# Attention scores of a hybrid encoder block: q_hi times k_lo of two heads on the two halves of TensorE's rows

## The chip, the cores and the metric

The kernel runs on one NeuronCore of a Trainium2 chip. The metric is the device time of one launch in microseconds (us), taken as the median of three runs. TensorE is called PE below, its weight loads PEld, VectorE is DVE, ScalarE is ACT, GpSimd is POOL and SyncE is SP.

## What is computed

One encoder layer on x of 1 x 1024 x 1024 in float32, with 8 query heads, 2 key/value heads and a head width of 64:

```
h = rmsnorm(x);  q | k | v | u = h @ w_in
q = axial_rope(rmsnorm(q));  k = axial_rope(rmsnorm(k))
s = q . k * 64**-0.5;  a = softmax(s) . v          # per 128-query block and head
p = pool_mixer(u)
x = x + concat([a, p]) @ w_out
x = x + (silu(h2 @ w_gate) * (h2 @ w_up)) @ w_down # h2 = rmsnorm(x)
```

The softmax runs over all 1024 keys; four query heads share one key/value head. D_FF is 2816.

## The kernel before

All matmuls take operands in a rounded 32-bit form (fp32r). To keep float32 accuracy each operand is split in a high part (the rounded value) and a low part (what is left), and a product is made of hi.hi, hi.lo and lo.hi. A matmul streams 512 columns through 128 rows.

For the scores, the split is stacked in the 128 rows instead: a head is 64 wide, so a query tile holds q_hi in rows 0 to 63 and q_lo in rows 64 to 127 (`prep_q` splits, `turn_q` transposes on PE and ACT copies the result out of PSUM, L804). The key side, `kT[:, kv, b, :]`, holds k_hi twice (b = 0, on both halves of the rows) and k_lo twice (b = 1). A head's scores for 128 queries and 1024 keys are then four matmuls in `score_part` (L828): two halves c of the keys, and for each b = 0 and b = 1, summed in a PSUM tile of two banks from `bank2` (two such tiles). q_lo times k_lo is summed as well. One call of `score_part` is a "part": two matmuls; two parts make a head, eight parts a unit (t, kv) of four heads, and there are 16 units. After a head's second part `weigh` lets DVE take the row maximum (L837) and ACT the exponential with its sum (L839), which frees the PSUM tile; `normalise` divides on POOL (L847).

The kernel uses eight PSUM banks: four single ones (`bank`, "b1") and two pairs ("b2"). In the attention loop a step s, with c = s % 8, issues in this order: `trans` for step s + 1 (four PE transposes into a single bank, then ACT takes the high part, L340, and DVE the low part, L349, which frees the bank); `score_to(s + lead)`, lead = 13, so part s + 13, which is also where `prep_q` and `turn_q` of the next query tile are called; `folded` at c = 1; `OutProj.run(K["out"][c])` (L908, three matmuls for each unit of `out`, from the second query tile on; its single bank is held from c = 3 to c = 7 and freed by DVE, L918); `av` (L871), whose single bank is held from c = 0 until `folded` of the next unit. Thirteen parts are made before, among the q projection's steps (L601); the last 13 steps make none.

PE's order is the program's order. The other engines' order is set when the program is built: `Flow` keeps jobs with estimated costs and due times, and gives out each engine's next instruction by due time; `flow.claim` picks the PSUM bank whose reader is done first; six rehearsals are made and the order of the best is taken. `split` picks the engine for each piece by the planner's estimate.

`K` is the table of places: "next_prep" and "next_turn" are the part (of the 16 of two units) after or before which the next tile's `prep_q` and `turn_q` are issued.

Of the kernel before, what the change touches and what calls it, by code (L numbers as in the profile page):

```python
# [10 lines left out]
F32 = mybir.dt.float32  # L11
F32R = mybir.dt.float32r
BF16 = mybir.dt.bfloat16
I32 = mybir.dt.int32
AF = mybir.ActivationFunctionType
# [3 lines left out]
P = 128  # L19
S = 1024  # L20
D = 1024
NT = S // P
NK = D // P
HD = 64
NQ = 8
NKV = 2
AW = NQ * HD
# [20 lines left out]
    "pieces": 1, "groups": [[0], [1], [2, 3], [4, 5, 6, 7]], "take": [0, 3], "tables": 2, "spread": [1],  # L48
    "ahead": [22, 39], "turn_k": 50, "wq": [60], "mix": [56, 62, 10, 30], "prep_q": [20], "turn_q": [33],
    "wo": [33, 39, 52, 62], "score": [36, 37, 38, 39, 47, 47, 52, 54, 57, 59, 61, 63, 63], "fold": 1,  # L50
    "out": [0, 0, 0, 2, 1, 2, 1, 2], "wo2": [3, 9, 10, 10, 16, 16], "mix_c": 5, "norm": 6, "next_prep": 8,
    "next_turn": 9, "lead": 13, "rehearsals": 6, "leave": 2,
    "load": {"x": 0.0, "pool": 0.0, "q": 0.0, "first": 0.0, "rest": 0.0, "turn": 0.4, "plain": 0.0, "blocks": 0.0},
    "down": [0.0] * 7, "wide": 2,
}
# [208 lines left out]
def act(n, extra=0.0):  # L264
    return "A", 0.1 + 0.00097 * n + extra


def dve(n):

    return "D", max(0.16, 0.07 + 0.00119 * n)  # L270


def dve_sbuf(n):
    return *dve(n), True


def dve_copy(n):
    return "D", max(0.16, 0.07 + 0.00056 * n), True
# [6 lines left out]
def pool_scale(n):  # L285
    return "G", 0.1 + 0.00103 * n, True
# [3 lines left out]
def block_kernel(  # L290
# [4 lines left out]
    nc = tc.nc  # L295

    def sb(stack, name, bufs=1, side=None):
        return stack.enter_context(tc.tile_pool(name=name, bufs=bufs, side=side, reuse_waits="tile"))
# [20 lines left out]
    o = EDGE  # L319
# [5 lines left out]
    flow = Flow(ranks)  # L325
    ffn = []

    def bank(dt=F32):
        flow.claim("b1", 4)
        return ps1.tile([P, 512], dt, tag="b1", name="b1")  # L330

    def bank2(dt=F32):
        flow.claim("b2", 2)
        return ps2.tile([P, 1024], dt, tag="b2", name="b2")

    def split(hi, lo, src, n, both=False):
        way = flow.quicker(act(n), dve_copy(n), pool_scale(n)) if both and not ffn else act(n)
        yield way
        if way[0] == "A":
            nc.scalar.activation(hi, src, AF.Copy)  # L340
        elif way[0] == "D":
            nc.vector.tensor_copy(hi, src)
        else:
            nc.gpsimd.tensor_scalar(hi, src, 1.0, 1.0, op0=ALU.mult, op1=ALU.mult)
        if both:
            yield from combine(n, lo, src, hi.bitcast(F32), ALU.subtract)
        else:
            yield dve(n)
            nc.vector.tensor_tensor(lo, src, hi.bitcast(F32), op=ALU.subtract)  # L349

    def combine(n, dst, a, b, op):

        way = flow.quicker(dve_sbuf(n), pool(n))
        yield way
        (nc.gpsimd if way[0] == "G" else nc.vector).tensor_tensor(dst, a, b, op=op)  # L355
# [20 lines left out]
    qp = qp_pool.tile([P, NT, D], F32, name="qp")  # L376
# [6 lines left out]
    identr = held.tile([P, P], F32R, name="identr")  # L383
# [5 lines left out]
    kT = sb(keys, "kT").tile([P, NKV, 2, S], F32R, name="kT")  # L389

    def work(dt=F32, n=D):
        return wk.tile([P, n], dt, tag="wk", name="wk")
# [89 lines left out]
    kv_job, kt_job, q_job = {}, {}, {}  # L482
# [290 lines left out]
    wo, qT, pn, mix, po, pts, osb, attn_job = [], {}, {}, {}, {}, {}, {}, {}  # L773
# [9 lines left out]
    def prep_q(t):  # L783
        qs = work(F32R).rearrange("p (h b d) -> p h b d", h=NQ, b=2)

        def parts():
            yield [q_job[t]]
            yield from split(qs[:, :, 0, :], qs[:, :, 1, :], qp[:, t, 0:AW].rearrange("p (h d) -> p h d", d=HD), AW, both=True)

        ready = flow.add(parts())  # L790
        dst = work(F32R)
        qT[t] = [dst]
        return ready, qs, dst

    def turn_q(t):
        ready, qs, dst = prepared[t]
        pt = bank2(F32R)
        flow.tensor(0.68, ready)
        for j in range(8):
            nc.tensor.transpose(pt[:, j * P:(j + 1) * P], qs[:, j].rearrange("p c d -> p (c d)"), identr)  # L800

        def evacuate():
            yield act(1024)
            nc.scalar.activation(dst, pt.bitcast(F32), AF.Copy)  # L804

        job = flow.add(evacuate())
        qT[t].append(job)
        flow.hold("b2", job)

    def prep_mix(t):  # L810
        mix[t] = [work(F32R).rearrange("p (k s) -> p k s", s=P) for _ in range(2)]
# [7 lines left out]
    sbank = {}  # L819

    def score_part(t, kv, i):
        h, c = 4 * kv + i // 2, i % 2
        if c == 0:
            sbank[0] = bank2()
        s = sbank[0]
        flow.tensor(0.462, qT[t][1], *([kt_job[j] for j in range(4 * c, 4 * c + 4)]))
        for b in range(2):
            nc.tensor.matmul(s[:, c * 512:(c + 1) * 512], qT[t][0][:, h * P:(h + 1) * P], kT[:, kv, b, c * 512:(c + 1) * 512], start=(b == 0), stop=(b == 1))  # L828
        if c == 0:
            return  # L830
        pe = work()
        sm = small.tile([P, 1], F32, tag="sm", name="sm", bufs=4)

        def weigh():
            nm = small.tile([P, 1], F32, tag="nm", name="nm", bufs=4)
            yield dve(S)
            nc.vector.tensor_reduce(nm, s, axis=AX, op=ALU.max, negate=True)  # L837
            yield act(S, 0.15)
            nc.scalar.activation(pe, s, AF.Exp, bias=nm, accum_out=sm)  # L839

        def normalise(first):
            yield [first]
            rs = small.tile([P, 1], F32, tag="rsm", name="rsm", bufs=4)
            yield dve_sbuf(1)
            nc.vector.reciprocal(rs, sm)  # L845
            yield pool_scale(S)
            nc.gpsimd.tensor_scalar(pe, pe, rs, 1.0, op0=ALU.mult, op1=ALU.mult)  # L847

        first = flow.add(weigh())
        flow.hold("b2", first)  # L850
        pn[t, h] = pe, flow.add(normalise(first))
# [89 lines left out]
    def score_to(p):  # L941
        while made[0] <= min(p, parts - 1):
            m = made[0]
            t, i = divmod(m, 16)
            if i == K["next_prep"] and t + 1 < NT:
                prepared[t + 1] = prep_q(t + 1)
            score_part(*units[m // 8], m % 8)
            made[0] += 1
            if i == K["next_turn"] and t + 1 < NT:
                turn_q(t + 1)  # L950
# [17 lines left out]
    def after(jobs):  # L968
        yield jobs
# [120 lines left out]
    raws, ready, done = {}, [], {}  # L1090
# [102 lines left out]
    class Passed:  # L1193

        done, ready = False, float("inf")
# [366 lines left out]
    for t in range(NT):  # L1562
        for _ in q_tile(t):
            for w in range(2):
                if K["mix"][2 + w] == step:
                    run(pool_mix(order[2 + w]))
            if at("prep_q", step):
                prepared[0] = prep_q(0)
            if at("turn_q", step):
                turn_q(0)  # L1570
            for _ in range(at("wo", step)):
                load_wo()
            for _ in range(at("score", step)):
                score_to(made[0])
            step += 1
# [72 lines left out]
    for p in range(1, NF // 2):  # L1648
        b = 2 * p
# [59 lines left out]
```

## Time and profile before

| what | value |
|---|---|
| time before, median of 3 runs | 1089.58 us (1088.71 to 1090.32) |
| the profiled execution's own time | 1089.24 us |
| its span in the profile | 1087.5 us |
| PE busy in the span | 1066.2 us (98%), 5114 matmuls |
| PEld busy | 877.6 us (81%) |
| DVE, ACT, POOL busy | 742.9, 492.9, 467.1 us |
| score matmuls (L828) | 256, from 127.9 to 392.5 us |

The span is what lies between the first and the last instruction in the trace; the time of the execution is 1.7 us longer. Busy PE time overlaps from one matmul to the next, so the distance between the starts of matmuls tells what one costs, not the length of its record.

### The profile page before, as it was taken

What the parts mean: (1) busy time and instruction counts of PE and PEld (TensorE: products, weight loads), DVE (VectorE), ACT (ScalarE), POOL (GpSimd) and SP (SyncE); (2) the same over time, 40 slices, a digit from 0 to 9 for tenths busy, and PEclk for the clock granted to TensorE, in tenths of its full rate; (3) what the DMA queues carried; (4) which work ended last, traced back from release to release, by engine and by line L of the source; (5) the groups of instructions that cost most, each with busy time, mean ns of one, the idle gap of its engine ahead of it and who ended that gap; (6) DMA issues with size and microseconds to landing.
All of it is one profiled execution on the core that took longest, in us unless ns stands there. A gap on an engine that the chain in (4) does not pass through costs nothing.

```text
span 1087.5 us, 13912 instructions
## 1 busy us (share of the span) xinstructions
PE 1066.2 (98%) x5114; PEld 877.6 (81%) x5114; DVE 742.9 (68%) x1228; ACT 492.9 (45%) x877; POOL 467.1 (43%) x380
## 2 busy tenths in 40 slices
PE   7999899999999999999999999999999999999998
PEld 7887777888888888878788887888788878888787
DVE  7888788787776766784974379346944496448745
ACT  6413257666665654634433433434333433343340
POOL 1263455443323223444643455355634464446431
PEclk9999999999999999999999999999999999999999
DMA  7122111000000000130022101220212012110114
GB/s 258 30 78 78 39 39 39 20 21 19 12 20 10 30 27 26 56 107 29 20 97 78 39 20 58 78 78 1 78 59 96 2 39 97 58 39 19 41 58 155
DMA packets 42564, 58.48 MB, mean 54 GB/s; under 512 B 4224, under 2 KB 32768, under 8 KB 42496
## 3 DMA queue, kind: packets, MB, share of 16 engines
q1 hardware_dynamic: 42496, 57.59, 15.8%
q8 instruction: 40, 0.66, 0.2%
q14 instruction: 28, 0.23, 0.1%
HBM read 53.39 MB, written 4.19 MB: 53 GB/s over the span
## 4 chain that ended last, share of the span: by engine, by line
PE 68%; DVE 9%; issue 3%; POOL 3%; ACT 1%; POOLq 0%; ACTq 0%
PE b L1176 36%; PE b L908 8%; PE b L1494 8%; PE b L871 5%; PE b L858 4%; PE b L828 4%; DVE wk L355 2%; DVE ring L355 2%; PE b L1441 2%; DVE qp L1456 2%; POOL wk L355 2%; POOL ring L355 1%; DVE raw L355 1%; PE b L881 1%; DVE wk L1045 1%
## 5 line engine op out<-in xcount | busy, mean ns | idle before, releaser
L1176 PE MATMUL b<-wk,ring 128*128 128x512 f32 x1872 | 426.4, 389 | 0.9 <-POOL ring L355 0.7
L1176 PEld LDWEIGHTS b<-wk,ring 128*128 128x128 f32 x1872 | 351.0, 188 | 74.7 <-POOL ring L355 1.1
L847 POOL TENSOR_SCALAR wk<-wk,rsm 128x1024 f32<-128x1024 f32 x64 | 76.4, 1202 | 151.4 <-DVE rsm L845 58.7
L355 POOL TENSOR_TENSOR ring<-raw,ring 128x512 fp32r<-128x512 f32 x54 | 70.0, 1297 | 157.8 <-ACT ring L340 138.8
L340 ACT ACTIVATE ring<-raw 128x512 fp32r<-128x512 f32 x130 | 81.6, 629 | 119.2 <-PE b L1176 57.1
L349 DVE TENSOR_TENSOR wk<-b,wk 128x512 fp32r<-128x512 f32 (+1 forms) x160 | 102.2, 658 | 45.5 <-ACT wk L340 45.0
L340 ACT ACTIVATE wk<-b 128x512 fp32r<-128x512 f32 (+1 forms) x160 | 90.3, 576 | 89.9 <-PE b L858 73.0
L1494 PE MATMUL b<-raw,ring 128*128 128x512 f32 x480 | 115.2, 394 | 4.1 <-DVE raw L355 2.5
L1494 PEld LDWEIGHTS b<-raw,ring 128*128 128x128 f32 x480 | 88.5, 188 | 29.2 <-DVE qp L1456 5.9
L355 DVE TENSOR_TENSOR ring<-raw,ring 128x512 fp32r<-128x512 f32 x76 | 57.8, 761 | 77.2 <-ACT ring L340 77.2
L1456 DVE TENSOR_TENSOR qp<-qp,b 128x512 f32<-128x512 f32 (+1 forms) x157 | 101.9, 675 | 9.0 <-PE b L1441 8.9
L908 PE MATMUL b<-wk 128*128 128x512 f32 x384 | 102.5, 397 | 0.0
L828 PE MATMUL b<-kT,wk 128*128 128x512 f32 x256 | 89.1, 430 | 0.1
L837 DVE TENSOR_REDUCE nm<-b 128x1 f32<-128x1024 f32 x64 | 78.0, 1218 | 13.4 <-PE b L828 12.4
L1494 PE MATMUL b<-wk,ring 128*128 128x512 f32 x360 | 85.2, 392 | 0.2
L871 PE MATMUL b<-wk,vv 128*128 128x512 f32 x256 | 82.3, 399 | 1.5 <-DVE wk L349 1.5
L908 PEld LDWEIGHTS b<-wk 128*128 128x128 f32 x384 | 70.7, 188 | 14.9
L355 POOL TENSOR_TENSOR ring<-silu,ring 128x512 fp32r<-128x512 f32 x35 | 54.1, 1547 | 63.3 <-ACT ring L340 63.3
L1494 PEld LDWEIGHTS b<-wk,ring 128*128 128x128 f32 x360 | 67.2, 188 | 16.6 <-DVE ring L355 1.8
L858 PEld LDWEIGHTS b<-ident,wk 128*128 128x128 f32 x512 | 63.6, 140 | 17.8 <-POOL wk L847 1.2
L858 PE MATMUL b<-ident,wk 128*128 128x128 f32 x512 | 76.9, 272 | 0.8 <-POOL wk L847 0.8
L839 ACT ACTIVATE wk<-b,nm 128x1024 f32<-128x1024 f32 x64 | 71.2, 1113 | 9.2 <-DVE nm L837 8.8
(145 smaller groups left out, 1451.3 us busy)
## 6 DMA issues: line engine op xcount, KB each, us to landing
raw<-in_w_gate_dram SPq DMA_DIRECT2D x22, 512.0 KB, 3.5
raw<-in_w_up_dram SPq DMA_DIRECT2D x22, 512.0 KB, 3.6
wk<-in_w_down_dram SPq DMA_DIRECT2D x20, 512.0 KB, 4.5
raw<-in_w_in_dram SPq DMA_DIRECT2D x10, 512.0 KB, 4.4
qp<-in_x_dram SPq DMA_DIRECT2D x8, 512.0 KB, 8.3
raw<-in_w_out_dram SPq DMA_DIRECT2D x8, 512.0 KB, 3.5
out_dram<-qp SPq DMA_DIRECT2D x15, 256.0 KB, 2.0
raw<-in_x_dram SPq DMA_DIRECT2D x14, 256.0 KB, 2.7
```

Of the source, the lines that this page charges most:

```text
L340: nc.scalar.activation(hi, src, AF.Copy)
L349: nc.vector.tensor_tensor(lo, src, hi.bitcast(F32), op=ALU.subtract)
L355: (nc.gpsimd if way[0] == "G" else nc.vector).tensor_tensor(dst, a, b, op=op)
L828: nc.tensor.matmul(s[:, c * 512:(c + 1) * 512], qT[t][0][:, h * P:(h + 1) * P], kT[:, kv, b, c * 512:(c + 1) * 512], start=(b == 0), stop= ...
L837: nc.vector.tensor_reduce(nm, s, axis=AX, op=ALU.max, negate=True)
L847: nc.gpsimd.tensor_scalar(pe, pe, rs, 1.0, op0=ALU.mult, op1=ALU.mult)
L858: nc.tensor.transpose(pt[:, j * P:(j + 1) * P], pe[:, c * P:(c + 1) * P], ident)
L871: nc.tensor.matmul(po[t, kv], vt, ps[:, b], start=(c == 0 and b == 0), stop=(c == NT - 1 and b == 1))
L908: nc.tensor.matmul(self.py, mix[self.t][a][:, k, :], wo[k][b][:, self.cs], start=(self.i == 0 and i == 0), stop=(self.i == NK - 1 and i == 2))
L1176: nc.tensor.matmul(bank_, w[0][:, a, i], x[:, b], start=(start and i == 0 and j == 0), stop=(stop and i == PARTS - 1 and j == 2), skip_gro ...
L1456: nc.vector.tensor_tensor(dst, dst, src, op=op)
L1494: nc.tensor.matmul(banks[t][0], x[:, a, t * P:(t + 1) * P], y[:, b], start=(own == name and i == 0 and j == 0), stop=(i == 1 and j == 2), ...
```

## The change

Q is laid out so that for even heads q_hi is in rows 0 to 63 and q_lo in rows 64 to 127, and for odd heads the other way round. The product with k_lo then takes q_hi alone: for the two heads of a pair it is four matmuls of 64 rows each, even head on rows 0 to 63, odd head on rows 64 to 127, alternating, each head into its own PSUM tile. The product with k_hi stays a matmul of 128 rows. Of each four parts, the first now issues nothing, the second claims both PSUM tiles and issues the four half matmuls, the third and fourth finish one head each with two full matmuls and start its softmax. q_lo times k_lo is no longer summed. `prep_q` splits even and odd heads apart (four instructions of 256 columns instead of two of 512). `turn_q` uses two single banks, four transposes and one copy of 512 columns each, instead of one two-bank tile. "next_prep" goes from 8 to 6, "next_turn" from 9 to 12.

```diff
-    "out": [0, 0, 0, 2, 1, 2, 1, 2], "wo2": [3, 9, 10, 10, 16, 16], "mix_c": 5, "norm": 6, "next_prep": 8,
-    "next_turn": 9, "lead": 13, "rehearsals": 6, "leave": 2,
+    "out": [0, 0, 0, 2, 1, 2, 1, 2], "wo2": [3, 9, 10, 10, 16, 16], "mix_c": 5, "norm": 6, "next_prep": 6,
+    "next_turn": 12, "lead": 13, "rehearsals": 6, "leave": 2,
...
-            yield from split(qs[:, :, 0, :], qs[:, :, 1, :], qp[:, t, 0:AW].rearrange("p (h d) -> p h d", d=HD), AW, both=True)
+            src = qp[:, t, 0:AW].rearrange("p (g o d) -> p g o d", o=2, d=HD)
+            for o in range(2):
+                yield from split(qs[:, o::2, o, :], qs[:, o::2, 1 - o, :], src[:, :, o], AW // 2, both=True)
...
     def turn_q(t):
         ready, qs, dst = prepared[t]
-        pt = bank2(F32R)
-        flow.tensor(0.68, ready)
-        for j in range(8):
-            nc.tensor.transpose(pt[:, j * P:(j + 1) * P], qs[:, j].rearrange("p c d -> p (c d)"), identr)
-        def evacuate():
-            yield act(1024)
-            nc.scalar.activation(dst, pt.bitcast(F32), AF.Copy)
-        job = flow.add(evacuate())
-        qT[t].append(job)
-        flow.hold("b2", job)
+        jobs = []
+        for i in range(2):
+            pt = bank(F32R)
+            flow.tensor(0.34, ready)
+            for j in range(4):
+                nc.tensor.transpose(pt[:, j * P:(j + 1) * P], qs[:, 4 * i + j].rearrange("p c d -> p (c d)"), identr)
+            def evacuate(i, pt):
+                yield act(512)
+                nc.scalar.activation(dst[:, i * 512:(i + 1) * 512], pt.bitcast(F32), AF.Copy)
+            jobs.append(flow.add(evacuate(i, pt)))
+            flow.hold("b1", jobs[-1])
+        qT[t].append(flow.add(after(jobs)))
...
     def score_part(t, kv, i):
-        h, c = 4 * kv + i // 2, i % 2
-        if c == 0:
-            sbank[0] = bank2()
-        s = sbank[0]
-        flow.tensor(0.462, qT[t][1], *([kt_job[j] for j in range(4 * c, 4 * c + 4)]))
-        for b in range(2):
-            nc.tensor.matmul(s[:, c * 512:(c + 1) * 512], qT[t][0][:, h * P:(h + 1) * P], kT[:, kv, b, c * 512:(c + 1) * 512], start=(b == 0), stop=(b == 1))
-        if c == 0:
+        pair, sub = divmod(i, 4)
+        h = 4 * kv + 2 * pair
+        if sub == 0:
             return
+        if sub == 1:
+            sbank[0], sbank[1] = bank2(), bank2()
+            flow.tensor(0.5, qT[t][1], *(kt_job[j] for j in range(NT)))
+            for c in range(2):
+                for o in range(2):
+                    r = slice(o * HD, (o + 1) * HD)
+                    nc.tensor.matmul(sbank[o][:, c * 512:(c + 1) * 512], qT[t][0][r, (h + o) * P:(h + o + 1) * P], kT[r, kv, 1, c * 512:(c + 1) * 512], start=True, stop=False)
+            return
+        h += sub - 2
+        s = sbank[sub - 2]
+        flow.tensor(0.462)
+        for c in range(2):
+            nc.tensor.matmul(s[:, c * 512:(c + 1) * 512], qT[t][0][:, h * P:(h + 1) * P], kT[:, kv, 0, c * 512:(c + 1) * 512], start=False, stop=True)
```

## Rows read from the trace of the kernel before

**Rows 1.** The page's head: span, then busy time of each engine.
```profile
span 1087.5 us, 13912 instructions
PE 1066.2 (98%) x5114; PEld 877.6 (81%) x5114; DVE 742.9 (68%) x1228; ACT 492.9 (45%) x877; POOL 467.1 (43%) x380
```
**Rows 2.** Three stretches: length, PE, PEld, DVE, ACT, POOL busy; PEclk, DMA, GB/s.
```profile
121.00:153.00 32.00, 29.55 (x133) 24.40 (x134) 23.81 (x46) 12.17 (x20) 15.11 (x12) 0.95 0.16 55
153.00:187.00 34.00, 31.54 (x178) 23.78 (x177) 30.06 (x49) 26.03 (x47) 16.71 (x13) 1.00 0.12 43
187.00:397.00 210.00, 210.00 (x1162) 175.52 (x1161) 161.01 (x275) 134.94 (x250) 78.06 (x73) 1.00 0.06 20
```
**Rows 3.** All waits of PE from 120 to 400 us: total, times, longest.
```profile
PE b L800 <- DVE wk L355: 3.3, 1, 3.3
PE b L871 <- DVE wk L349: 1.5, 5, 0.4
PE b L858 <- POOL wk L847: 0.8, 1, 0.8
```
**Rows 4.** Groups of instructions, 153 to 400 us: count, busy us, mean ns, idle before.
```profile
L349 DVE TENSOR_TENSOR wk<-b,wk 128x512 fp32r<-128x512 f32 x133 | 89.2, 685 | 38.1 <-ACT wk L340 37.9
L828 PE MATMUL b<-kT,wk 128*128 128x512 f32 x231 | 81.8, 435 | 0.1
L908 PE MATMUL b<-wk 128*128 128x512 f32 x304 | 81.3, 395 | 0.0
L340 ACT ACTIVATE wk<-b 128x512 fp32r<-128x512 f32 x133 | 77.7, 597 | 73.4 <-PE b L858 65.1 <-PE b L871 7.2
L837 DVE TENSOR_REDUCE nm<-b 128x1 f32<-128x1024 f32 x59 | 71.8, 1218 | 7.6 <-PE b L828 6.6
...
L839 ACT ACTIVATE wk<-b,nm 128x1024 f32<-128x1024 f32 x59 | 65.7, 1113 | 2.8 <-DVE nm L837 2.3
...
L349 DVE TENSOR_TENSOR wk<-b,wk 128x256 fp32r<-128x256 f32 x14 | 5.8, 412 | 0.0
```
**Rows 5.** PE in order of time: start, length of the merged piece, line, count.
```profile
306.64 0.64 PE L871 MATMUL b<-wk,vv 128*128 128x512 f32 x2
...
307.47 0.71 PE L828 MATMUL b<-kT,wk 128*128 128x512 f32 x2
308.02 1.55 PE L908 MATMUL b<-wk 128*128 128x512 f32 x6
...
310.21 0.71 PE L828 MATMUL b<-kT,wk 128*128 128x512 f32 x2
310.76 0.81 PE L800 MATMUL b<-identr,wk 128*128 128x128 f32 x8
311.40 0.92 PE L908 MATMUL b<-wk 128*128 128x512 f32 x3
...
317.43 0.60 PE L858 MATMUL b<-ident,wk 128*128 128x128 f32 x4
317.78 0.70 PE L828 MATMUL b<-kT,wk 128*128 128x512 f32 x2
318.32 1.55 PE L908 MATMUL b<-wk 128*128 128x512 f32 x6
```
**Rows 6.** PE's weight loads in order of time, two loads of the scores.
```profile
302.85 0.30 PEld L828 LDWEIGHTS b<-kT,wk 128*128 128x128 f32 x2
```
**Rows 7.** ACT in order of time, idle before in brackets.
```profile
311.66 1.03 ACT L804 ACTIVATE wk<-b 128x1024 fp32r<-128x1024 f32 x1 [0.51 <-PE b L800]
...
318.06 0.60 ACT L340 ACTIVATE wk<-b 128x512 fp32r<-128x512 f32 x1 [1.40 <-PE b L858]
318.56 1.11 ACT L839 ACTIVATE wk<-b,nm 128x1024 f32<-128x1024 f32 x1
```
**Rows 8.** DVE in order of time, a row maximum that found DVE idle.
```profile
310.96 1.22 DVE L837 TENSOR_REDUCE nm<-b 128x1 f32<-128x1024 f32 x1 [0.96 <-PE b L828]
```
**Rows 9.** DVE at the first query tile's split.
```profile
120.57 2.82 DVE L355 TENSOR_TENSOR wk<-qp,wk 128x512 fp32r<-128x512 f32 x1
```

## The prediction

> **What bounds the kernel now.** The page's head comes first: PE is busy in 98% of the span [rows 1], so the question is whether the stretch with the scores is bound by PE too. The view by stretches answers it in three parts [rows 2]. From 187 to 397 us, where output projection, transposes, scores and values are woven together, PE is busy in all 210 us while DVE has 161 and ACT 135: every us of PE work taken out or put in moves the end. From 153 to 187, the first query tile, which has no output projection between, PE lacks 2.5 us and DVE is busy 30 of 34: there DVE sets much of the pace. From 121 to 153 PE works except at the start. PE's waits say the same: one of 3.3 us for the first query tile's split, 1.5 us in five pieces for a low part, 0.8 us for POOL, and none for a PSUM tile of the scores [rows 3]. After 400 us nothing is changed but the planner's order, and I give that nothing.
>
> **What one matmul costs.** Six matmuls of the output projection last 1.55 us together and one record 0.395 [rows 4, 5], so the starts are (1.55 - 0.395) / 5 = 0.23 us apart. The loads of weights hide behind the matmul ahead: two loads of the scores take 0.30 us and one about 0.19, so loads can follow at 0.11 us [rows 6].
>
> **The half pass.** Removed: per pair of heads four full matmuls, 4 x 0.23 = 0.92 us. Added: four half matmuls. No half matmul is in this trace, so bounds. If the two halves do not run together, they cost 0.92 again. If they run together and start together, two rounds are 2 x 0.23 = 0.46. In between, each half has its own load: lane a starts at 0, lane b 0.11 later, and the second round ends at 0.46 + 0.11 = 0.57. I take 0.57, since the loads are the one serial thing that the rows price: 0.35 saved.
>
> **The change of shape, twice per pair.** PE goes from 128 rows to halves and back. Lower bound nothing: from transposes to scores to transposes again [rows 5] the starts show no gap. Upper bound: PE empties, the record's tail 0.395 - 0.23 = 0.165, and the load is exposed, 0.11: 0.275 each. I take 0.11, the exposed load alone. The saving is then 0.35 - 0.22 = 0.13 us a pair, between -0.20 (emptied) and 0.46 (free, and started together); if the halves run one after the other it is -0.22 with my value.
>
> The Trainium skill, "TensorEngine Tiling (Array Packing)", Key Properties, says that changing the tiling mode drains TensorE, and that tiles otherwise load and multiply in parallel. No row here shows a drain. By it the sum would go to the upper bound, a rival below.
>
> Which pairs count: 32 pairs. Three are made in the q projection and 25 from the second query tile on, where PE is the bound [rows 2]; four (parts 13 to 28) in the first tile's steps, where I give them nothing. 28 x 0.13 = **3.6 us saved** (from -5.6 to 12.9).
>
> **Turning q.** Before, eight transposes take 311.40 - 310.76 = 0.64 us in a two-bank tile, and PE goes on at once [rows 5]. Now part 12 falls in step s % 16 = 15, so c = 7. Of the four single banks one is held by `av` until the next fold, one by the output projection until the end of this very step, and one was just filled by this step's `trans`. One is left. The first four transposes fit; the second four wait until a bank is read. With T the start of `trans` (317.43 in rows 5; the scores at 317.78 fall away, part 12 being empty): transposes until T + 0.43, first half of q until T + 0.75. ACT starts on the high part of `trans` at T + 0.63 and is done with it at about T + 1.13 (318.06 and 318.56 [rows 7]); then q's first copy of 0.6 (L340's mean for 512 columns [rows 4]) frees its bank at about T + 1.73. The bank of `trans` comes later, as DVE's 0.69 follows. PE waits 1.73 - 0.75 = 1.0. Lower bound, if ACT were free: 0.09 to start (L804 after the transposes' end at 311.57) + 0.6 + a little = 0.75; upper, if the exponential is put first and the bank of `trans` is the one: 1.2. I take 0.95. Behind the waiting transposes stand six output matmuls, `av`, and all that follows in PE's order. It happens for six tiles (the turn made in the first tile's steps finds the output projection's bank free): 6 x 0.95 = **5.7 us lost** (4.5 to 7.2).
>
> **Both PSUM tiles at once.** Part 1 of a pair claims the tiles of both heads before, so the odd head's softmax must be over one empty part later. From the end of its matmuls to the freed tile: 0.20 (310.76 to 310.96 [rows 5, 8]) + 1.22 + 0.09 + 1.11 [rows 4] = 2.6 us, if neither engine is busy. From the second tile on, the tighter claim is at c = 4: in the old times 306.64 to 310.21 is 3.57 us, less the scores of c = 3 that are gone (308.02 - 307.47 = 0.55): 3.0 [rows 5]. That holds with 0.4 to spare, less than one L349 (0.69) or L340 (0.6) ahead in the queue. Twelve such claims, 0 to 0.3 each: I take **0.7 us** (0 to 3.6), near nothing, as the planner knows the due time. In the first tile's steps the gap is 3.0 less six output matmuls (1.38), 1.6: every one of four claims comes up to 1.0 short. But DVE, the bound there, gets no more work, and part of its queue is worked off while PE waits: 0 to 4, I take **1.5 us**.
>
> **Splitting q in four.** Only the first tile's split has PE waiting (3.3 us [rows 3]). Two DVE pieces of 256 cost 2 x 0.41 against 0.69 [rows 4]: 0.14, and one more hand-over of some 0.25; **0.4 us**. But that subtract took 2.82 us instead of 0.69 [rows 9], held up by something on its way; in two pieces it may be held twice (+2.1) or get through (-2.1). The later splits hide in DVE's 49 and POOL's 132 idle us of the long stretch [rows 2].
>
> **Sum.** -3.6 + 5.7 + 0.7 + 1.5 + 0.4 = +4.7 us on the profiled execution's 1089.24 (span 1087.5 and 1.7 around it): 1093.9, given as **1094**. That execution lies 0.34 below the median 1089.58, within the runs' spread. About 0.2% (2.2 us) is what a measurement of this kernel can tell from no change.
>
> **Rivals.** (1) Faster: changing between halves and full costs nothing and both lanes start together. Then 28 x 0.46 = 12.9 against the 8.3 of waits: 1084.6. It decides from a saving of (8.3 + 2.2) / 28 = 0.38 a pair. For it: loads do run ahead of matmuls [rows 6], and transposes and matmuls alternate without a gap [rows 5]; against it: four loads at 0.11 in 0.46 us leave no slack. Chance 0.28. The Trainium skill, "TensorE: Matmul & The Clock Gate", Part 3, gives this outcome, tiles starting about 4 ns apart; no run here shows it yet.
>
> (2) The emptied array, 0.275 a change: 28 x 0.20 = 5.6 more work, +13.9 with the waits: 1103. For it the long tail of each record, against it that no row shows the array empty itself. Chance 0.08. (3) The change doesn't do what it says, the halves run in turn: 32 x 0.22 = 7.0, +15.3: 1104.5. No row speaks for or against. Chance 0.06. (4) The saving and the waits cancel (a saving of 0.22 to 0.37 a pair, or turning q without the wait): 1087.4 to 1091.8. Chance 0.15.
>
> **How the numbers follow.** The forecast has the remaining 0.43, with its own range 1091.8 to 1100. Faster 0.28, same 0.15, slower 0.43 + 0.08 + 0.06 = 0.57. The range 1083 to 1102 leaves out the fastest part of (1) (some 0.07) and most of (2) and (3).
>
> **What would show it.** The half matmuls' pieces: starts in pairs 0.11 apart or less and a piece from first half to next full matmul of 0.7 to 0.8 us prove the step; 0.5 proves (1), over 1.0 proves (2) or (3). In PE's waits six entries of about 1 us ahead of the second four transposes of q, released by ACT's copy; and waits of PE for L839 at c = 4 and in the first tile's steps. PE busy in the long stretch should fall below its length for the first time. Wrong it is if PE's list has no wait at the turns, or the halves' piece is near 0.5.

## The result, and the profile after

The changed kernel takes 1097.37 us (median of 4 runs, 1096.61 to 1099.16) against 1089.71 for the kernel before beside it: ratio 1.0077 [1.0065, 1.0089], so 7.7 us slower. It was predicted slower, at 1094.0 with a range to 1102. The span of its profiled execution is 1095.4 us, 7.9 more than before.

In the changed kernel most lines stand four to fourteen further down: the half matmuls are L838, the full score matmuls L844, the turn of q L804 and its copies L808, row maximum L851, exponential L853, transposes of the probabilities L872, values L885, output projection L922. Five landmarks cut the span. "Early" ends at the first `trans` (152.93 us before, 149.04 after), "first tile" runs from there to the first output matmul (187.32 and 188.87), "long" from there to the sixteen transposes behind the last scores (429.71 and 437.70), and the rest follows. As part 12 is empty now, 24 score matmuls stand in the early stretch where 26 stood, and the long stretch holds 192 where it held 190: about 0.5 us of work has moved from the first row of the table to the third.

| stretch | before, us | after, us | difference |
|---|---|---|---|
| early | 152.93 | 149.04 | -3.9 |
| first tile | 34.39 | 39.83 | +5.4 |
| long | 242.39 | 248.83 | +6.4 |
| rest of the span | 657.8 | 657.7 | 0 |

The head of the page and the stretches, after (columns as in [rows 1, 2]):

```profile
span 1095.4 us, 13962 instructions
PE 1068.1 (98%) x5114; PEld 865.3 (79%) x5114; DVE 745.7 (68%) x1222; ACT 500.9 (46%) x903; POOL 469.3 (43%) x384
```

```profile
121.00:153.00 32.00, 29.71 (x143) 22.70 (x144) 23.22 (x46) 17.43 (x30) 21.01 (x15) 1.00 0.20 66
153.00:187.00 34.00, 29.30 (x154) 21.33 (x153) 27.24 (x45) 24.25 (x45) 18.60 (x15) 0.95 0.12 39
187.00:397.00 210.00, 205.47 (x1130) 160.61 (x1130) 155.53 (x260) 134.00 (x256) 75.29 (x70) 1.00 0.05 16
```

From 187 to 397 PE was busy in all 210 us [rows 2]; now it lacks 4.5, as forecast. PE's share of the whole span is 98% in both, which tells nothing. The waits of PE from 115 to 420 us, after (total, times, longest), name what is missing:

```profile
PE b L804 <- ACT wk L808: 4.5, 5, 0.9
PE b L885 <- DVE wk L349: 3.4, 3, 1.3
PE b L804 <- DVE wk L355: 1.5, 2, 1.2
PE b L872 <- DVE wk L349: 1.4, 1, 1.4
PE b L804 <- DVE wk L349: 0.9, 1, 0.9
PE b L838 <- ACT wk L853: 0.3, 1, 0.3
```

The first row is the turn of q in five query tiles of the long stretch, the fifth its turn in the first tile's steps; the second, fourth and last row lie in the first tile as well. The third is the first query tile's split, 1.5 us where 3.3 stood [rows 3]. Beside the split's wait that makes 10.5 us where 2.3 stood before [rows 3].

PE in order of time, after: a half pass, and the turn of q.

```profile
307.84 0.60 PE L872 MATMUL b<-ident,wk 128*128 128x128 f32 x4
308.37 0.73 PE L838 MATMUL b<-kT,wk 64*128 64x512 f32 x4
309.03 0.73 PE L885 MATMUL b<-wk,vv 128*128 128x512 f32 x2
309.60 0.60 PE L872 MATMUL b<-ident,wk 128*128 128x128 f32 x4
...
322.89 0.54 PE L804 MATMUL b<-identr,wk 128*128 128x128 f32 x4
324.37 0.54 PE L804 MATMUL b<-identr,wk 128*128 128x128 f32 x4 [0.94 <-ACT wk L808]
```

The half pass takes 309.03 - 308.37 = 0.66 us to the next full matmul: four matmuls in less than three full ones would need (0.69), so the lanes do run together (0.7 to 0.8 was forecast). The same view cut to 308.30 to 308.40 us has two of the four already:

```profile
308.37 0.50 PE L838 MATMUL b<-kT,wk 64*128 64x512 f32 x2
```

Both halves of a round start together, within the 0.03 us that this cut leaves; the other two start together at 308.70. But the transposes ahead take 0.53 where they took 0.35 before a full score matmul [rows 5], and the two value matmuls behind take 0.57 instead of 0.46. At the turn, 1.48 us lie between the starts of the two groups of four transposes, of which the first group's work is some 0.36.

**A ledger of the long stretch.** With each piece of PE counted from its start to the next piece's start, waits included, over all pieces of the long stretch:

| PE's work, us | before | after | after, q turned at part 15 | after, halves made full rows |
|---|---|---|---|---|
| scores | 51.84 | 42.31 | 42.02 | 50.61 |
| transposes of the probabilities | 38.24 | 42.46 | 42.62 | 38.32 |
| values | 50.64 | 53.72 | 53.42 | 52.25 |
| output projection | 90.24 | 93.08 | 93.08 | 91.81 |
| turn of q | 3.20 | 9.09 | 3.19 | 9.07 |
| the rest | 8.23 | 8.17 | 8.16 | 8.26 |

(The last two columns are experiments 1 and 2.) Before to after, scores save 9.53 us, though two matmuls more fall in the stretch. The three lines below take back 4.22 + 3.08 + 2.84 = 10.14. The turn adds 5.89. The half pass, seen in its own rows alone, is a plain gain; it pays in the rows beside it.

### The profile page after: what moved, and what is told of

The parts are those of the page before. It is cut to its first block, busy times and chain, and to the rows that moved or that the text cites. A ratio compares the mean times of both kernels' runs of the same rounds, so it can differ in the third digit from the quotient of the medians.

```text
span 1095.4 us, 13962 instructions
## 1 busy us (share of the span) xinstructions
PE 1068.1 (98%) x5114; PEld 865.3 (79%) x5114; DVE 745.7 (68%) x1222; ACT 500.9 (46%) x903; POOL 469.3 (43%) x384
## 4 chain that ended last, share of the span: by engine, by line
PE 79%; DVE 11%; issue 4%; POOL 3%; ACT 3%; DMA 1%; SPq 0%; ACTq 0%; POOLq 0%; DVEq 0%
PE b L1190 36%; PE b L922 8%; PE b L1508 8%; PE b L885 5%; PE b L872 4%; PE b L684 4%; PE b L601 3%; DVE wk L355 3%; PE b L844 2%; PE b L838 2%; POOL wk L355 2%; PE b L1455 2%; PE b L490 2%; DVE qp L1470 2%; DVE ring L355 1%
## 5 line engine op out<-in xcount | busy, mean ns | idle before, releaser
L355 POOL TENSOR_TENSOR ring<-raw,ring 128x512 fp32r<-128x512 f32 x46 | 59.5, 1293 | 146.9 <-ACT ring L340 133.3
L355 DVE TENSOR_TENSOR ring<-raw,ring 128x512 fp32r<-128x512 f32 x84 | 67.1, 800 | 75.9 <-ACT ring L340 75.5
L922 PE MATMUL b<-wk 128*128 128x512 f32 x384 | 105.4, 405 | 0.0
L885 PE MATMUL b<-wk,vv 128*128 128x512 f32 x256 | 86.0, 413 | 3.4 <-DVE wk L349 3.4
L853 ACT ACTIVATE wk<-b,nm 128x1024 f32<-128x1024 f32 x64 | 71.3, 1116 | 28.9 <-DVE nm L851 25.7
L851 DVE TENSOR_REDUCE nm<-b 128x1 f32<-128x1024 f32 x64 | 76.8, 1216 | 11.2 <-PE b L844 11.1
L922 PEld LDWEIGHTS b<-wk 128*128 128x128 f32 x384 | 68.4, 189 | 16.7 <-issue 4.4
L872 PE MATMUL b<-ident,wk 128*128 128x128 f32 x512 | 77.2, 273 | 1.4 <-DVE wk L349 1.4
L872 PEld LDWEIGHTS b<-ident,wk 128*128 128x128 f32 x512 | 63.8, 141 | 17.7 <-DVE wk L349 1.7
L340 ACT ACTIVATE ring<-silu 128x512 fp32r<-128x512 f32 x60 | 37.3, 629 | 84.3 <-PE b L1508 29.4
L355 POOL TENSOR_TENSOR wk<-wk 128x512 fp32r<-128x512 f32 (+2 forms) x45 | 64.2, 1436 | 23.8 <-ACT wk L340 9.8
```

The lines of the kernel that those rows point to most:

```text
L872: nc.tensor.transpose(pt[:, j * P:(j + 1) * P], pe[:, c * P:(c + 1) * P], ident)
L885: nc.tensor.matmul(po[t, kv], vt, ps[:, b], start=(c == 0 and b == 0), stop=(c == NT - 1 and b == 1))
L922: nc.tensor.matmul(self.py, mix[self.t][a][:, k, :], wo[k][b][:, self.cs], start=(self.i == 0 and i == 0), stop=(self.i == NK - 1 and i == 2))
```

## The experiments

**1. The turn of q at part 15** instead of 12, in the changed kernel, so that it falls into a step without a full set of taken banks.

```diff
-    "next_turn": 12, "lead": 13, "rehearsals": 6, "leave": 2,
+    "next_turn": 15, "lead": 13, "rehearsals": 6, "leave": 2,
```

> The changed kernel with q turned after part 15 instead of part 12, so in a step with c = 2, where the output projection holds no bank. Theory (the wait for a single bank in the middle of the turn costs 1.2 us in each of six tiles): 7 us less than the changed kernel's 1097.4, so 1090 to 1092, and no wait of the second four transposes left in PE's list. Rival (the two copies of 512 columns and the transposes crowd ACT wherever they stand, and the wait only moves): 1095 to 1098, with other waits of about the same sum.

Measured: 1095.01 us (1092.2 to 1097.55), ratio 1.0053 [1.0034, 1.0072]; the profiled execution took 1092.2. The long stretch fell from 248.83 to 242.49, and the time from turn to turn from 35.69 to 34.53: the turn costs 1.16 us a tile. PE's waits of this kernel, 115 to 420 us:

```profile
PE b L885 <- DVE wk L349: 4.3, 5, 1.7
PE b L838 <- ACT wk L853: 3.6, 3, 2.1
PE b L804 <- DVE wk L355: 1.5, 2, 1.2
```

No wait for L808 is left, so the cause of the long stretch's loss is shown. The median time is another matter: 1095.01 lies at the edge of the rival's range. The profiled execution had a granted clock of 1.00 over its span of 1090.0 us; the other three had 0.994 to 0.997 and spans of 1092.6 to 1095.4, and no trace of them shows where. In the profiled one the first tile took 40.74 us, 0.9 more than after: the second row is the claim of both PSUM tiles, waiting for the exponential of the pair before. With the turn's waits gone the long stretch is at 242.49 against 242.39 before, with the two score matmuls more in it; from turn to turn, where the work is equal, a tile takes 34.53 us against 34.59. So the half passes themselves gain next to nothing there.

**2. The halves made full rows:** everything as after, with the first product of each pair as four matmuls of 128 rows.

```diff
-                    r = slice(o * HD, (o + 1) * HD)
+                    r = slice(0, P)
```

This sums q_lo times k_lo as well.

> The changed kernel with the four half matmuls of a pair made full ones again (128 rows, both q_hi and q_lo against k_lo), all else as changed. Theory (the half pass takes 0.87 us with its two changes of shape, four full ones 0.92): slower than the changed kernel by 28 x 0.06 = 1.5 us, 1097.5 to 1100. Rival (the half pass is worth what the two lanes promise, 0.35 us a pair or more, and the loss lies wholly in the waits): 1107 or more.

Measured: 1099.82 us, ratio 1.0098 [1.0083, 1.0113], 2.4 over after. PE in order of time, this kernel:

```profile
309.78 0.60 PE L872 MATMUL b<-ident,wk 128*128 128x128 f32 x4
310.14 1.17 PE L838 MATMUL b<-kT,wk 128*128 128x512 f32 x4
311.15 0.62 PE L885 MATMUL b<-wk,vv 128*128 128x512 f32 x2
311.61 0.60 PE L872 MATMUL b<-ident,wk 128*128 128x128 f32 x4
```

Set beside the same four rows of after, this prices the half pass: transposes 0.36 against 0.53, the four matmuls 1.01 against 0.66, values 0.46 against 0.57. From transposes to transposes it is 1.83 against 1.76: the halves save 0.35, the change into them costs 0.17 and out of them 0.11, and 0.07 is left a pair. From turn to turn it is 35.94 against 35.69, 0.06 a pair. The theory held and the rival, that the lanes save much more, fell. The ledger's last column shows another thing: this kernel without the turn's 5.87 extra is still 2.1 us above before, with no half matmul in it. About 0.5 of this is the two score matmuls more. The output line's 1.57 is mostly moved, not added: an empty part lets output matmuls follow transposes directly, and then six of them take 1.47 instead of 1.38 us; the score part that used to stand there carried that 0.09 (0.55 for two matmuls against 2 x 0.23), and four matmuls in one part carry it once where two parts carried it twice. What is left, some 1.5, is in the values' line: seven pieces of two value matmuls take 0.64 us and five 0.57, where 0.46 is usual. Behind one of 0.64, VectorE and PE in order of time in this kernel:

```profile
278.03 2.35 DVE L851 TENSOR_REDUCE nm<-b 128x1 f32<-128x1024 f32 x2
280.29 0.68 DVE L349 TENSOR_TENSOR wk<-b,wk 128x512 fp32r<-128x512 f32 x1
```

```profile
280.73 0.80 PE L885 MATMUL b<-wk,vv 128*128 128x512 f32 x2
281.37 0.60 PE L872 MATMUL b<-ident,wk 128*128 128x128 f32 x4
```

The two row maxima of a pair stand ahead of the low part, which ends at 280.97; the second value matmul needs it and starts some 0.18 us late. As the first one's record is still running, no list of waits has this.

**3. The half pass done twice** in the changed kernel (the scores then hold it twice).

```diff
-            for c in range(2):
+            for n, c in enumerate((0, 1, 0, 1)):
...
-                    nc.tensor.matmul(sbank[o][:, c * 512:(c + 1) * 512], qT[t][0][r, (h + o) * P:(h + o + 1) * P], kT[r, kv, 1, c * 512:(c + 1) * 512], start=True, stop=False)
+                    nc.tensor.matmul(sbank[o][:, c * 512:(c + 1) * 512], qT[t][0][r, (h + o) * P:(h + o + 1) * P], kT[r, kv, 1, c * 512:(c + 1) * 512], start=True, stop=n < 2)
```

> The changed kernel with each half pass made twice (the second overwrites the first with the same sums). It adds four half matmuls per pair without another change of shape. Theory (lanes run side by side, but each round of two lasts 0.33 us since its loads are not hidden): 0.66 us a pair, 32 pairs, up to 21 us more, less where PE waits anyway: 1112 to 1119. Rival 1 (two lanes side by side at 0.23 a round, the rest being the changes of shape): 0.46 a pair, 15 us or less, 1107 to 1112. Rival 2 (lanes in turn): 0.92 a pair, 26 to 29 us, 1123 or more.

Measured: 1113.05 us, ratio 1.0223 [1.0203, 1.0243]; the long stretch is 11.25 over after, 0.47 for each of the 24 pairs in it. PE in order of time:

```profile
318.43 1.19 PE L838 MATMUL b<-kT,wk 64*128 64x512 f32 x8
319.55 0.50 PE L885 MATMUL b<-wk,vv 128*128 128x512 f32 x1
```

Eight half matmuls take 1.12 us, four 0.66: two more rounds cost 0.46, so a round of two halves costs what one full matmul costs, 0.23. My theory (0.66 again) fell and the first rival held; the time alone could not tell, as 1113.05 lies in the theory's range and 1 us above that rival's. The lanes are fully side by side; what a single short pass loses, it loses at its two ends.

**4. The order of the halves:** even, even, odd, odd instead of alternating.

```diff
-            for c in range(2):
-                for o in range(2):
+            for o in range(2):
+                for c in range(2):
```

> The changed kernel with the four half matmuls in the order even, even, odd, odd instead of alternating. Theory (two halves on different rows run side by side, two on the same rows one after the other): only the middle two can overlap, so the piece grows by one round of 0.23 us a pair: 25 to 32 pairs, 5 to 7.5 us slower than the changed kernel, 1102 to 1105. Rival (the lanes don't overlap, or the chip finds the overlap in any order): within 1.5 us of 1097.4.

Measured: 1098.26 us (1097.31 to 1102.95), ratio 1.0089 [1.0070, 1.0107]; 248.93 in the long stretch, 0.1 over after. PE in order of time:

```profile
308.70 0.74 PE L838 MATMUL b<-kT,wk 64*128 64x512 f32 x4
309.37 0.73 PE L885 MATMUL b<-wk,vv 128*128 128x512 f32 x2
```

The piece is 0.67 us, as with alternation. The theory, that the order written makes the lanes overlap, fell: here the order made no difference.

**5. Only the turn changed,** in the kernel before: two single banks at part 12, with the split at part 6, full score matmuls throughout.

```diff
-    "next_turn": 9, "lead": 13, "rehearsals": 6, "leave": 2,
+    "next_turn": 12, "lead": 13, "rehearsals": 6, "leave": 2,
...
-        pt = bank2(F32R)
...
+        for i in range(2):
+            pt = bank(F32R)
```

("next_prep" goes to 6 too, and the rest of `turn_q` is as in the change.)

> The kernel before, scores head by head, with only q's turn in two single banks and the two places moved (6 and 12), as in the change. Theory (the second four transposes wait for a single bank, 1.2 us in five tiles and about as much in the sixth): five or six such waits in PE's list and 5 to 8 us slower than before, 1094 to 1097. Rival (the waits come only together with pairs): 1088 to 1091.

Measured: 1097.34 us, ratio 1.0071 [1.0055, 1.0086]: as slow as the whole change, without one half matmul. PE's waits, 115 to 420 us:

```profile
PE b L802 <- DVE wk L349: 3.5, 5, 0.7
PE b L802 <- DVE wk L355: 3.4, 1, 3.4
PE b L860 <- ACT wk L806: 2.3, 2, 1.8
...
```

The turn waits again, for the bank of `trans` this time (first row). The composition differs from after: the first query tile's wait of 3.4 us is still there, the first tile takes 39.73, the long stretch 246.80.

**6. Single banks alone:** as 5, but at parts 8 and 9, where the kernel before has its split and turn.

```diff
-        pt = bank2(F32R)
...
+        for i in range(2):
+            pt = bank(F32R)
```

> The kernel before with q turned in two single banks, at the old places (8 and 9). Theory (the single banks alone make PE wait, wherever the output projection holds one): 0.8 to 1.2 us a tile from the second tile on, 5 to 7 us in all, 1094 to 1097, with the first tile's stretch at 34 to 36 us. Rival (the wait belongs to the place after part 12): 1089 to 1091.

Measured: 1093.83 us, ratio 1.0045 [1.0031, 1.0059]; 35.47 us from turn to turn against 34.59, so 0.88 a tile; long stretch 246.82, first tile 34.80. PE's waits at the turn:

```profile
PE b L802 <- DVE wk L349: 3.6, 5, 0.7
```

The single banks make the wait, at either of these two places (not after part 15, as experiment 1 shows). The first tile is unharmed here, which is what sets 6 apart from 5.

**7. The first tile's pairs undone:** the changed kernel with the turn at part 15 and, for parts 12 to 27, full matmuls for each head as before (this sums q_lo times k_lo there).

```diff
+ALONE = (12, 28)
...
+        if ALONE[0] <= 8 * units.index((t, kv)) + i < ALONE[1]:
+            return score_alone(t, kv, i)
```

> The changed kernel with q turned after part 15, and with parts 12 to 27 (all made in the first query tile's steps, where no output projection stands between) made head by head with full matmuls, as before the change. Theory (the pairs cost the first tile's stretch 5.4 us, because both PSUM tiles are claimed with too little work between; the early stretch keeps its 3.9 us): the stretch from the first transposes to the first output projection back at 34 to 35 us, and 1085 to 1087 in all. Rival (that stretch is long because DVE has come to it with a backlog from the shorter one before): it stays at 38 us or more, 1090 to 1094.

Measured: 1092.45 us, ratio 1.0032 [1.0021, 1.0043]. The first tile still took 40.41 us: the theory that the pairs lengthen it fell, though the pair of parts 28 to 31, which also lies in that stretch, stayed a pair. Another wait stands there, for the low part:

```profile
PE b L902 <- DVE wk L350: 6.1, 6, 3.5
```

Its longest piece, 3.5 us up to 182.10, has this behind it (VectorE and GpSimd in order of time):

```profile
176.69 2.54 POOL L356 TENSOR_TENSOR wk<-raw,wk 128x1024 fp32r<-128x1024 f32 x1
176.92 3.39 DVE L356 TENSOR_TENSOR wk<-raw,wk 128x1024 fp32r<-128x1024 f32 x1
```

Two subtracts of weights, one on each engine, start 0.23 us apart; the one on VectorE takes 3.39 us where the same shape takes 1.20 and 1.21 elsewhere in that run, and the low part is queued behind it and a row maximum.

**8. The split at part 8,** with the turn at part 15, in the changed kernel.

```diff
-    "out": [0, 0, 0, 2, 1, 2, 1, 2], "wo2": [3, 9, 10, 10, 16, 16], "mix_c": 5, "norm": 6, "next_prep": 6,
-    "next_turn": 12, "lead": 13, "rehearsals": 6, "leave": 2,
+    "out": [0, 0, 0, 2, 1, 2, 1, 2], "wo2": [3, 9, 10, 10, 16, 16], "mix_c": 5, "norm": 6, "next_prep": 8,
+    "next_turn": 15, "lead": 13, "rehearsals": 6, "leave": 2,
```

> The changed kernel with q turned after part 15 and the next tile's split back at part 8 (from 6). Theory (the first tile's longer stretch, which stays at 40 us even without pairs there, comes from the split's earlier place, which crowds DVE and POOL with the end of the q projection): the stretch from the first transposes to the first output projection falls from 40 to 35 or 36 us, 1086 to 1090 in all. Rival (it comes from the earlier end of the stretch before: DVE's and POOL's work up to there is the same, and what is gained early is waited for later): 39 us or more and 1091 to 1096.

Measured: 1091.61 us, ratio 1.0027 [1.0017, 1.0037]. First tile 42.05, long stretch 242.56. The theory that the earlier split disturbs the first tile fell.

**9. The split at part 6 in the kernel before.**

```diff
-    "out": [0, 0, 0, 2, 1, 2, 1, 2], "wo2": [3, 9, 10, 10, 16, 16], "mix_c": 5, "norm": 6, "next_prep": 8,
+    "out": [0, 0, 0, 2, 1, 2, 1, 2], "wo2": [3, 9, 10, 10, 16, 16], "mix_c": 5, "norm": 6, "next_prep": 6,
```

> The kernel before with nothing but the next tile's split at part 6 instead of 8. Theory (the split's place crowds the first tile's stretch): the stretch grows from 34.4 towards 39 us and the kernel is 3 to 5 us slower, 1092 to 1095. Rival (the place is harmless): 1089 to 1091, stretch 34 to 35 us.

Measured: 1089.62 us, ratio 1.0006 [0.9996, 1.0015], first tile 34.58: moving the split alone costs nothing.

**10. The split in four, in the kernel before.**

```diff
-            yield from split(qs[:, :, 0, :], qs[:, :, 1, :], qp[:, t, 0:AW].rearrange("p (h d) -> p h d", d=HD), AW, both=True)
+            src = qp[:, t, 0:AW].rearrange("p (g o d) -> p g o d", o=2, d=HD)
+            for o in range(2):
+                yield from split(qs[:, o::2, 0, :], qs[:, o::2, 1, :], src[:, :, o], AW // 2, both=True)
```

> The kernel before with only the split of q in four instructions of 256 columns (even and odd heads apart), in the old layout. Theory (in the changed kernel this took the first tile's wait from 3.3 to 1.5 us and the stretch at half clock behind it away): 3 to 4 us faster than before, 1086 to 1087, with PEclk 1.00 from 121 to 153 us. Rival (the early gain came from the pairs or from the earlier place of the split): within 1 us of before, 1089 to 1090.5.

Measured: 1090.71 us, ratio 1.0010 [1.0000, 1.0019]. The wait is still there, so the split is not what gained 3.9 us early on. VectorE, GpSimd and PE in order of time in this kernel, and then VectorE and GpSimd in the changed kernel:

```profile
121.07 2.34 POOL L355 TENSOR_TENSOR wk<-raw,wk 128x1024 fp32r<-128x1024 f32 x1 [2.70 <-ACT wk L340]
121.10 2.59 DVE L355 TENSOR_TENSOR wk<-qp,wk 128x256 fp32r<-128x256 f32 x1
123.74 0.80 PE L802 MATMUL b<-identr,wk 128*128 128x128 f32 x7 [3.43 <-DVE wk L355]
```

```profile
121.39 0.41 DVE L355 TENSOR_TENSOR wk<-qp,wk 128x256 fp32r<-128x256 f32 x1
124.46 2.40 POOL L355 TENSOR_TENSOR wk<-raw,wk 128x1024 fp32r<-128x1024 f32 x1 [6.18 <-ACT wk L340]
```

The same piece of q takes 2.59 us where it runs beside GpSimd's subtract of a weight, and 0.41 where the planner put that subtract 3 us later. The Trainium skill, "SBUF — State Buffer", section "SBUF: two separate sides", says that a VectorE operation with two inputs in SBUF and a GpSimd operation that reads SBUF lock each other out for the whole instruction; the 2.59 beside 2.34 agrees.

**11. The subtract moved in the kernel before:** its first output weight loaded at step 37 instead of 33.

```diff
-    "wo": [33, 39, 52, 62], "score": [36, 37, 38, 39, 47, 47, 52, 54, 57, 59, 61, 63, 63], "fold": 1,
+    "wo": [37, 39, 52, 62], "score": [36, 37, 38, 39, 47, 47, 52, 54, 57, 59, 61, 63, 63], "fold": 1,
```

> The kernel before with one load of output weights issued four steps later in the q projection (step 37 instead of 33), so that POOL's 1024-column subtract for it falls behind the first query tile's split on DVE. Theory (the 3.3 us wait of PE at 120 us comes from that POOL instruction running beside DVE's subtract, which then takes 2.82 instead of 0.68 us): the wait falls to 1.5 us or less, the half clock behind it goes, 1085.5 to 1087. Rival (the split is late by its own queue): within 1 us of before.

Measured: 1088.05 us, ratio 0.9984 [0.9976, 0.9993]: 1.7 us faster than before, the fastest version seen, though within 0.2%. The profiled execution, at 1089.2, has none of the gain. PE's wait, and VectorE and GpSimd around it:

```profile
PE b L800 <- DVE wk L355: 2.3, 1, 2.3
```

```profile
119.70 2.92 DVE L355 TENSOR_TENSOR wk<-wk 128x256 f32<-128x256 f32 x2
119.70 2.64 POOL L355 TENSOR_TENSOR wk<-raw,wk 128x1024 fp32r<-128x1024 f32 x1
```

The subtract did not leave; one of the same shape stands 0.8 us earlier, beside two other VectorE subtracts, which take 2.92 us. (The changed kernel's two take 0.75 at 118.90.) So the theory was not put to the test.

**12. That, with the first weight's subtract kept off GpSimd.**

```diff
-        wo.append((hi, lo, consume(tok, flow.add(split(hi, lo, raw, D, both=True), at))))
+        wo.append((hi, lo, consume(tok, flow.add(split(hi, lo, raw, D, both=k > 0), at))))
```

> The kernel before with the first load of output weights at step 37 and its split on ACT and DVE instead of the planner's choice, so that POOL has no 1024-column subtract while DVE splits the first query tile. Theory (that POOL instruction holds DVE up): PE's wait at 120 us falls from 3.3 us to 1.5 or less, the half clock behind it goes, and 2 to 4 us are gained, 1086 to 1088. Rival (what is gained early is lost again in the first tile's stretch, which DVE paces): the wait falls, the stretch behind grows, 1088.5 to 1090.5.

Measured: 1088.95 us, ratio 0.9996 [0.9987, 1.0005], with 2.5 us of the wait left and no gain over before. Here too a GpSimd subtract runs beside VectorE's at that time:

```profile
118.44 3.04 DVE L355 TENSOR_TENSOR wk<-wk 128x256 f32<-128x256 f32 x2
118.79 2.41 POOL L355 TENSOR_TENSOR wk<-raw,wk 128x1024 fp32r<-128x1024 f32 x1
```

So no run shows what the kernel before would take without that meeting.

## Why the prediction came out as it did

The direction and the range held; the size was 7.7 where 4.7 was forecast. Term by term, against the span's +7.9:

| term | predicted | measured |
|---|---|---|
| half passes and their changes of shape | -3.6 | 0 in the long stretch (+0.5 with two score matmuls more) |
| turning q | +5.7 | +7.0 |
| claim of both tiles at c = 4 | +0.7 | 0 |
| first tile, without the turn in it | +1.5 | +4.3 |
| split in four, with all that is early | +0.4 | -3.4 (-3.9 with two score matmuls less) |

That the time fell within the range was partly luck: the terms missed by +3.6, +1.3, -0.7, +2.8 and -3.8, and an early gain that the sum did not hold made up for what the half pass did not give.

- **The half pass** was the step that failed: 3.6 was forecast and next to nothing came. Its parts were near: 0.35 saved by four halves, as forecast, though not for the reason given (the lanes are not 0.11 apart but start together, a pass's first round takes 0.33 us and a later one 0.23), and 0.28 for the two changes where 0.22 was taken. That leaves 0.07 of the 0.13. What the working did not have at all is the other half of the edit: gathering four matmuls in one part and leaving one part empty cost some 1.5 us over the long stretch with full matmuls (experiment 2), and the halves win back 1.5. The "no gap" that I read between transposes and scores [rows 5] hid a price of 0.09 inside the scores' own 0.55, and it moved to whatever follows the transposes.
- **Turning q** was right as a mechanism. Six waits of 0.9 stand in PE's list. Five are in the long stretch, with ACT's copy of the first half as the releaser, as told; the sixth is in the first tile's steps, where the prediction expected a free bank. (Its six tiles without that one were a miscount: there are five.) Over the long stretch the price is 5.89 / 5 = 1.18 us a turn by the ledger and 1.16 by experiment 1, against 0.95, within its bounds of 0.75 and 1.2. Experiments 5 and 6 show that it does not depend on the pairs.
- **The claim at c = 4** was free: no wait of PE for L853 stands in the long stretch. In the first tile one of 0.3 us does.
- **The first tile** was under-sized, beyond its bound of 4. In the changed kernel the low part is late there. VectorE in order of time:

```profile
155.10 2.34 DVE L851 TENSOR_REDUCE nm<-b 128x1 f32<-128x1024 f32 x2
157.36 1.28 DVE L349 TENSOR_TENSOR wk<-b,wk 128x512 fp32r<-128x512 f32 x2
```

  and PE behind it:

```profile
158.09 0.50 PE L885 MATMUL b<-wk,vv 128*128 128x512 f32 x1 [1.30 <-DVE wk L349]
```

  A pair ends both its heads close together, so two row maxima of 1.2 us stand ahead of the low part, and PE waits 1.3 us; the same stands at 162.53 and 165.53. The prediction spoke of DVE getting no more work, which is true, and not of its order. In all, PE's waits in this stretch went from 2.3 [rows 3] to 6.0 us, and a spell at the lower clock cost about 1.7 (windows below); together that is the 5.4. What sets these off is less clear: with the pairs undone (experiment 7) the stretch stayed at 40.4.
- **The early part** was worth 3.9 us, and the prediction had named the 2.82 us subtract as held up by something, with 2.1 either way. The something is GpSimd's subtract, by the same piece with and without it in experiment 10; no run took that subtract alone away. That the wait shrank by 1.8 explains less than half. The clock is most of the rest, and 0.5 is the two score matmuls that moved. Windows of the kernel before, then of the changed one:

```profile
124.00:128.00 4.00, 4.00 (x14) 3.19 (x14) 2.77 (x9) 1.02 (x1) 0.00 (x0) 0.57 0.16 43
```

```profile
122.00:128.00 6.00, 6.00 (x31) 4.54 (x31) 2.30 (x12) 2.98 (x4) 3.54 (x3) 1.00 0.03 4
...
174.00:180.00 6.00, 5.66 (x21) 3.88 (x22) 5.29 (x7) 3.93 (x8) 4.48 (x4) 0.72 0.18 51
```

  Before, PE's granted clock behind the long wait was 0.57 of full speed for 4 us, mostly the lower of its two levels (1.2 and 2.4 GHz), worth some 4 x 0.43 = 1.7 us of work; after, it was 1.00 there. The lower clock came back in the first tile: 0.72 from 174 to 180 us, and 6 x 0.28 = 1.7 us were lost again there.

Of the rivals, the free change with lanes together (1084.6) was right about the lanes and wrong about the change. By the Trainium skill, "TensorE: Matmul & The Clock Gate", Part 3, tiles on different rows start almost together; the two that start at 308.37 agree. By the Trainium skill, "TensorEngine Tiling (Array Packing)", Key Properties, changing the tiling mode drains TensorE. The 0.17 into the halves and 0.11 out of them are less than the 0.275 each that the rival of the emptied array took; no run here tells a drain from an exposed load of weights. That the halves run in turn is excluded.

**Open:** why the first tile takes 39.7 us or more in every kernel that turns q after part 12 or 15 (after, and experiments 1 to 5, 7 and 8: 39.7 to 42.7), and 34.4 to 34.9 in every one that turns it after part 9. Undoing the pairs does not bring it back (7), and neither the split's place (9) nor the single banks (6) lengthen it by themselves. Experiment 5 joins these two to the turn's place and is long, so what is left is that place, alone or together with them. The waits in it differ from kernel to kernel: row maxima ahead of the low part, two engines' weight subtracts at once, a bank of `trans`, and in most a spell of half clock. No version with the turn's place alone changed and nothing else was run.

## What to carry to other kernels

Price a matmul on part of the rows with its two neighbours: from the transposes ahead to the transposes behind, 0.35 us saved became 0.07, and a half pass pays only if more rounds stand together: a round of two halves saves 0.23, and 2 x 0.23 - 0.07 = 0.39 went for going in and out. Count what an edit does to the order of parts as well as what it does to the parts, with a ledger of start to next start over the whole stretch. And where a stage is tuned tight, look at which buffers are free at the very step to which work is moved: the turn of q cost more than the pass it made room for could give.

## What the runs showed that was not expected

- Value matmuls started up to 0.18 us late without any wait in PE's list, since the record of the matmul ahead was still running; only the ledger of starts shows it (experiment 2).
- A full score matmul behind fp32 transposes costs 0.09 us more than one behind its like: two take 0.55, not 0.46, and six output matmuls 1.47, not 1.38, when they follow transposes directly.
- Halves written even, even, odd, odd take 0.67 us, alternating ones 0.66.
- One GpSimd subtract of 128x1024 stretched a VectorE subtract that ran beside it from 0.41 to 2.59 us, and another from 1.21 to 3.39. Where the planner put it changed with edits that don't touch it: at 120.46 us before, at 124.46 in the changed kernel.
